# How many raw and split weights may be held: fixed numbers against the pages left free at each unit

## The chip, the cores and the metric

The kernel runs on one core of a Trainium2 chip. What counts is the device time of one execution in microseconds (us). Five engines matter: TensorE (PE) multiplies, VectorE (DVE) and ScalarE (ACT) prepare its operands and take its results, GpSimd (POOL) and SyncE (SP) issue transfers from memory (HBM) into the on-chip buffer. Each engine works through its own instructions in order and waits on semaphores for the others.

## The reference: what is computed

One layer of a streaming encoder over 256 tokens of width 2048, batch 1, all in float32:

```
x = LN(ALPHA * x + 0.5 * (silu(x @ w1) * (x @ w3)) @ w2)           first FFN, inner width 5632
proj = x @ w_in                                                   conv'd q, k; v; output gate; mLSTM gates;
                                                                  stick-breaking q, k, v; two branch gates ga, gb
y_m  = head_norm(mLSTM(q, k, v, gates)) * sigmoid(mo)             4 heads of 256
y_sb = stick_breaking(sq, sk, sv)                                 8 heads of 128
mix  = (sigmoid(ga) * (y_m @ w_up_m) + sigmoid(gb) * (y_sb @ w_up_sb)) @ w_out
x = LN(ALPHA * x + mix)
x = LN(ALPHA * x + 0.5 * second FFN)
x = x + sigmoid(x @ w_ple_gate) * (p @ w_ple_proj)
```

Nearly all of the arithmetic is products of the 256 rows of `x` with weight matrices. The weights are read from HBM once each, some 530 MB in all.

## The kernel before

**Weights and units.** A weight is a block of 256 rows by (mostly) 512 columns. It arrives as float32 in a *raw* page (512 KB, one load on SP's queue, L1251) and is split in two: ACT casts it to a rounded form, the high part (L1277), and DVE subtracts that from the raw values, which leaves the low part (L1281). The two parts are two *split* pages. A *unit* is the work of PE on one weight for 128 of the tokens: six matmuls of 128x128 by 512 columns, for each of the two row blocks high times high (L1333), high times low (L1334) and low times high (L1335). There are 1,528 units and 1,100 weights.

**Seven-product pairs.** Where two matrices with the same input are multiplied (w1 and w3; the two branch gates; halves of other parts of w_in), `seven` replaces eight block products by seven. Some of its weights are sums. A sum is made in place in a raw page, either by DVE (`plus`, L373) or by a transfer that POOL issues and that adds on landing (`plus_load`, L379); both are made from a raw page that an earlier weight of the pair has just been split from, so the addition cannot begin before that split. Each weight of such a pair has one unit; a plain weight (`group`) has two, one for each half of the tokens. The four pairs of the two branch gates are of this kind, like the nine pairs of each FFN.

**Pages.** All of this lives in one pool of 51 pages (`PAGES`): the residual (4 pages), the transposed activations in split form (`actT`, 2 token halves x 4 chunks = 8 pages for the plain form, 8 more for the sums that the seven products need), hidden chunks of the FFN (2 pages each), tiles of the mixer, the raws and the splits. A page that is given to a new tile cannot be written before the last reader of the old one is done; that wait sits on the engine or queue that writes first.

**Order.** The program is a list of units with plain functions between them. Main units (plain groups) and side units (seven-product pairs) are woven. The instruction streams are written in the order of this list: a clock of the builder, `sched.now`, goes forward by the units alone and sets when the smaller pieces of work (evacuations, transposes, attention steps) are written in between.

**How far ahead.** After each unit `splits_due` writes the splits of coming weights as long as fewer than a certain number are held; a split counts as held from the writing of its cast until its last unit. A weight that is needed and not yet split is split on the spot. Each `split_one` first writes the cast and the subtraction, then counts out the raw pages that this weight was the last to use, and then calls `loads`, which writes loads until a certain number of raws are held. The two numbers come from `HELD`, by the stretch of the program, and from `RAW_EDGE, SPLIT_EDGE` = 4, 11 near the two ends of an FFN and the mixer:

```
HELD = {"ffn": (11, 6), "mix": (6, 6), "woven": (9, 6), "wide": (11, 6), "late": (8, 5)}
while pos["load"] < most and pos["raw"] < (4 if pos["at"] < 6 else limits(pos["split"])[0]):     # loads
while pos["split"] < most and len(splits) < limits(pos["split"])[1]:                               # splits_due
```

"ffn" holds for both FFNs, "woven", "wide" and "late" for the three parts of the mixer's long middle, where the seven-product pairs of w_in run beside the rest, "mix" for what is left.

Of the kernel before, what the change touches and what calls it, by code (L numbers as in the profile page):

```python
# [24 lines left out]

PAGES = 51
TEMP_BUFS = 6


HELD = {"ffn": (11, 6), "mix": (6, 6), "woven": (9, 6), "wide": (11, 6), "late": (8, 5)}  # L30
RAW_EDGE, SPLIT_EDGE = 4, 11
EDGE = 6

# [1 line left out]
PSUM_BUFS = 8  # L35
# [151 lines left out]
    return [p[0] for p in pairs] + [p[1] for p in pairs]  # L187


@with_exitstack  # L190
def kernel(
    ctx: ExitStack,
    tc: tile.TileContext,
    x, p, ffn1_w1, ffn1_w3, ffn1_w2, ln1_g, ln1_b, w_in, b_gates_m, conv_m, norm_m,
    w_up_m, w_up_sb, w_out, ln2_g, ln2_b, ffn2_w1, ffn2_w3, ffn2_w2, ln3_g, ln3_b,
    w_ple_gate, w_ple_proj, out,
):
    nc = tc.nc
    x, out = x[0], out[0]
    p = p[0, 0]  # L200
    w_in, w_out, w_up_m, w_up_sb = w_in[0], w_out[0], w_up_m[0], w_up_sb[0]

    consts = ctx.enter_context(tc.tile_pool(name="consts", bufs=1))
    dram_pool = ctx.enter_context(tc.tile_pool(name="dram", bufs=1, space=bass.MemoryType.DRAM))
    page_pool = ctx.enter_context(tc.tile_pool(name="page", bufs=PAGES))
    temp_pool = ctx.enter_context(tc.tile_pool(name="temp", bufs=TEMP_BUFS))
    small = ctx.enter_context(tc.tile_pool(name="small", bufs=4))
    ps_pool = ctx.enter_context(tc.tile_pool(name="ps", bufs=PSUM_BUFS, space=bass.MemoryType.PSUM))
    ctx.enter_context(tc.manual_schedule())

    sched = Sched()
    temps = [0]
# [1 line left out]
    def temp():  # L214
        sched.until(lambda: temps[0] < TEMP_BUFS)
        temps[0] += 1
        return temp_pool.tile([P, COL], F32, name="temp", tag="temp")
# [44 lines left out]
    def load_x(c, t):  # L262
        nc.sync.dma_start(out=xres(t, c * COL), in_=x[t * P:(t + 1) * P, c * COL:(c + 1) * COL])
# [209 lines left out]
    class Norm:  # L473
        def __init__(self, g, b, act, scale, wait, away=None):
            self.g_in, self.b_in, self.act, self.scale, self.wait, self.away = g, b, act, scale, wait, away
            self.whole = set()
            self.stats, self.half = {}, {}
# [570 lines left out]
    def sb(*heads):  # L1048
        col0 = [(sq0 + h * DS, 2 * DS) for h in heads[::2]]
        return flat(group(w_in, range(0, D, 2 * P), col0, len(heads) * DS, x1T,  # L1050
                          lambda ps, t: sb_columns(ps, t, heads)))
# [33 lines left out]
    def half(g, h, last=False):  # L1085
        w, act = ((w_up_m, ymT), (w_up_sb, ysbT))[h]
        return flat(group(w, range(0, HM * DM, 2 * P), g * COL, COL, act, up_done(g, h, last)))

    def ups(g):
        return half(g, 0) + half(g, 1, True)  # L1090
# [17 lines left out]
    last = sb(14, 15)  # L1108
# [3 lines left out]
    late = [Mode("late")] + half(0, 1, True) + half(1, 1, True) + ups(2)  # L1112
# [114 lines left out]
    splits = {}  # L1227
    pos = {"load": 0, "split": 0, "at": 0, "raw": 0}

    def at_edge(j):  # L1230
        return any(-EDGE <= j - e < EDGE for e in edges)

    def limits(j):

        if at_edge(j):
            return RAW_EDGE, SPLIT_EDGE
        return HELD[[m for e, m in modes if e <= j][-1]]

    def pieces(j):
        return [slice(0, 1), slice(1, 2)] if j == 0 else [slice(0, 2)]  # L1240

    def loads(most=len(raws)):
        while pos["load"] < most and pos["raw"] < (4 if pos["at"] < 6 else limits(pos["split"])[0]):
            j = pos["load"]
            r = raws[j]
            r.tile = page_pool.tile([P, 2, COL], F32, name="raw", tag="page")
            for ks in pieces(j):
                at = 0
                for src in r.src:
                    n = src.shape[-1]  # L1250
                    nc.sync.dma_start(out=r.tile[:, ks, at:at + n], in_=src[:, ks])  # L1251
                    at += n
                if j == 0 and ks.start == 0:
                    load_x(0, 1)
            pos["load"] += 1
            pos["raw"] += 1
# [11 lines left out]
    def split_one():  # L1268
        j = pos["split"]
        w = weights[j]  # L1270
        make(j)
        assert w.made or not w.make
        r = w.raw.tile[:, :, :w.cols]
        splits[j] = [page_pool.tile([P, 2, COL], F32R, name="split", tag="page") for _ in range(2)]
        hi, lo = (h[:, :, :w.cols] for h in splits[j])
        for ks in pieces(j):
            nc.scalar.copy(hi[:, ks], r[:, ks])  # L1277
            make(j + 1)
            if weights[min(j + 1, len(weights) - 1)].made or not weights[min(j + 1, len(weights) - 1)].make:
                make(j + 2)  # L1280
            nc.vector.tensor_tensor(out=lo[:, ks], in0=r[:, ks], in1=hi[:, ks], op=ALU.subtract)  # L1281
        pos["split"] += 1
        for f in w.soon:
            assert f.raw.tile is not None
            f.make()
            f.made = True
        pos["raw"] -= len(w.frees)
        for r in w.frees:
            r.tile = None
        loads()  # L1290

    def splits_due():
        most = pos["at"] + 3 if pos["at"] < 8 else len(weights)
        while pos["split"] < most and len(splits) < limits(pos["split"])[1]:
            split_one()
            if at_edge(pos["split"]):
                break

    for c in range(4):
        if c == 0:  # L1300
            load_x(0, 0)
            loads(1)
        for t in range(TT):
            if c:
                load_x(c, t)
            sched.spawn(start(c, t), max(0.01 * t, 5.2 * c + 1.3 * t - 2.6))
        loads(2 * c + 2)
    sched.run()
    split_one()
    sched.now = 0.02  # L1310
    sched.run()
    splits_due()
    warm(WARM2)
    make_tri()
    for u in program:
        if isinstance(u, (Boundary, Mode)):
            continue
        if not isinstance(u, Unit):
            u()
            continue  # L1320
        sched.until(lambda: u.act.ready(u.chunk, u.tt))
        j = u.tile.index
        pos["at"] = max(pos["at"], j)
        while pos["split"] <= j:
            split_one()
        if u.start:
            u.acc["ps"] = ps_pool.tile([P, COL], F32, name="mm", tag="ps")
        ps = u.acc["ps"][:, :u.cols]
        a, w = u.act.tiles[u.chunk, u.tt], splits[j]
        for k in range(2):  # L1330
            hi, lo = a[:, 0, u.sub + k], a[:, 1, u.sub + k]
            first, last = u.start and k == 0, u.stop and k == 1
            nc.tensor.matmul(ps, hi, w[0][:, k, :u.cols], start=first, stop=False, skip_group_check=u.onto)  # L1333
            nc.tensor.matmul(ps, hi, w[1][:, k, :u.cols], start=False, stop=False, skip_group_check=u.onto)  # L1334
            nc.tensor.matmul(ps, lo, w[0][:, k, :u.cols], start=False, stop=last, skip_group_check=u.onto)  # L1335
        sched.now += 6 * 0.2161 * u.cols / COL
        u.tile.uses -= 1
        if u.tile.uses == 0:
            splits.pop(j)
        if u.stop:  # L1340
            u.done(ps, u.tt)
        sched.run()
        splits_due()
# [27 lines left out]
```

## Time and profile before

| | |
|---|---|
| three runs, median (lowest to highest) | 2167.77 us (2166.32 to 2170.53) |
| the profiled execution, its own time | 2172.74 us |
| its span on the core | 2171.1 us |
| PE busy in it | 2154.1 us (99%) |
| DVE, ACT, POOL busy | 1921.2 (88%), 1360.8 (63%), 227.8 us (10%) |
| granted clock of PE, mean | 0.999 |
| bytes moved | 540.16 MB, 249 GB/s over the span |

A busy share says how much of the span an engine had an instruction in work, not whether it was held up inside one; matmuls overlap, so that a busy PE is not yet a PE at its peak. A group of instructions is named by its line, engine and tiles; behind its count stand the busy time, the mean duration of one and the idle time of the engine just before them, with what ended most of that idle time. Two rows of L1333 belong to each unit, so the n-th pair of them dates the n-th unit.

### The profile page before, as it was taken

How to read it: one execution, taken by the hardware profiler on the slowest of the kernel's cores; microseconds unless marked ns; L12 is line 12 of the kernel's file. 1: busy time of each engine (PE TensorE's matmuls, PEld its weight loads, DVE VectorE, ACT ScalarE, POOL GpSimd, SP SyncE). 2: the span in 40 equal slices, each digit the busy share in tenths (PEclk: the TensorE clock that was granted, in tenths of full speed). 3: DMA queues.
4: the chain of work that ended last, by engine and by line, in shares of the span. 5: the costliest groups of instructions: out<-in, count | busy, mean ns of one | idle time of the engine just before them, and what ended most of it. 6: DMA issues, size and time to landing. Idle time of an engine off the chain costs nothing.

```text
span 2171.1 us, 27709 instructions
## 1 busy us (share of the span) xinstructions
PE 2154.1 (99%) x9774; PEld 1778.0 (82%) x9774; DVE 1921.2 (88%) x2122; ACT 1360.8 (63%) x1681; POOL 227.8 (10%) x194
## 2 busy tenths in 40 slices
PE   9999999999999999999999999999999999999999
PEld 7888888888888888888877888888888888887887
DVE  6899999999998898889889886799999999999974
ACT  7656666656665766678876563655656666556572
POOL 0111111111100000101110100011111111110000
PEclk9999999999999999999999999999999999999999
DMA  9899899999994667998988986679999999999642
GB/s 348 215 276 270 249 270 273 277 273 265 276 316 134 218 218 215 239 254 244 286 238 210 303 296 206 203 193 270 270 246 271 279 274 272 251 271 291 238 158 94
DMA packets 285355, 540.16 MB, mean 249 GB/s; under 512 B 17272, under 2 KB 34592, under 8 KB 285216
## 3 DMA queue, kind: packets, MB, share of 16 engines
q1 hardware_dynamic: 234624, 440.87, 59.8%
q0 software_dynamic: 50592, 97.53, 25.1%
q8 instruction: 76, 1.25, 0.2%
q14 instruction: 63, 0.52, 0.1%
HBM read 532.04 MB, written 6.29 MB: 248 GB/s over the span
## 4 chain that ended last, share of the span: by engine, by line
PE 87%; DVE 5%; DMA 3%; issue 3%; ACT 1%; POOL 0%; SPq 0%; DVEq 0%; POOLq 0%; ACTq 0%
PE mm L1334 28%; PE mm L1333 28%; PE mm L1335 28%; DMA raw<-in_ffn_w_dram 3%; DVE split L1281 3%; PE ms L300 1%; DVE raw L373 1%; ACT split L1277 1%; PE ms L526 0%; DVE temp L599 0%; POOL raw L379 0%; PE ms L913 0%; PE ms L928 0%; DVE big L651 0%; PE ms L991 0%
## 5 line engine op out<-in xcount | busy, mean ns | idle before, releaser
L1277 ACT CAST split<-raw 128x1024 fp32r<-128x1024 f32 (+1 forms) x1101 | 1099.4, 1043 | 538.4 <-DMA raw<-in_ffn_w_dram 194.2
L1281 DVE TENSOR_TENSOR split<-raw,split 128x1024 fp32r<-128x1024 f32 (+1 forms) x1101 | 1289.4, 1210 | 120.9 <-ACT split L1277 112.0
L1333 PE MATMUL mm<-split,actT 128*128 128x512 f32 (+1 forms) x3056 | 1199.2, 392 | 1.5 <-DVE big L427 1.4
L1334 PE MATMUL mm<-split,actT 128*128 128x512 f32 (+1 forms) x3056 | 1185.3, 388 | 4.2 <-DVE split L1281 4.2
L1335 PE MATMUL mm<-split,actT 128*128 128x512 f32 (+1 forms) x3056 | 1185.8, 388 | 0.6 <-DVE actT L307 0.6
L1334 PEld LDWEIGHTS mm<-split,actT 128*128 128x128 f32 x3056 | 574.9, 188 | 121.4 <-DVE split L1281 9.1
L1335 PEld LDWEIGHTS mm<-split,actT 128*128 128x128 f32 x3056 | 574.3, 188 | 120.8 <-DVE actT L307 1.4
L1333 PEld LDWEIGHTS mm<-split,actT 128*128 128x128 f32 x3056 | 574.8, 188 | 116.7 <-DVE big L427 1.6
L379 POOL DMA_DIRECT2D raw<-in_ffn_w_dram x140 | 169.8, 1439 | 1187.1 <-DVE split L1281 852.9
L373 DVE TENSOR_TENSOR raw<-raw 128x1024 f32<-128x1024 f32 x198 | 241.0, 1218 | 3.1 <-DMA raw<-in_w_in_dram 1.5
L379 POOL DMA_DIRECT2D raw<-in_w_in_dram x46 | 55.7, 1402 | 517.8 <-DVE split L1281 425.7
L651 DVE SCALAR_TENSOR_TENSOR big<-mm,big 128x512 f32<-128x512 f32 x112 | 76.2, 682 | 3.0 <-PE mm L1335 2.8
L302 ACT CAST actT<-ms 128x512 fp32r<-128x512 f32 x60 | 35.2, 587 | 66.8 <-PE ms L300 61.8
L599 DVE TENSOR_TENSOR temp<-mm,temp 128x512 f32<-128x512 f32 x108 | 73.0, 686 | 1.8 <-PE mm L1335 0.6
L307 DVE TENSOR_TENSOR actT<-ms,actT 128x512 fp32r<-128x512 f32 x60 | 41.0, 684 | 16.0 <-ACT big L306 11.6
L245 ACT ACTIVATE temp<-mm 128x512 f32<-128x512 f32 (+1 forms) x36 | 20.3, 570 | 48.2 <-PE mm L1335 48.2
L241 ACT ACT_TABLE_LOAD x34 | 43.6, 1283 | 0.6
L295 DVE TENSOR_TENSOR actT<-temp,actT 128x512 fp32r<-128x512 f32 x40 | 26.5, 687 | 17.4 <-ACT actT L294 17.3
L1193 DVE TENSOR_TENSOR temp<-temp,big 128x512 f32<-128x512 f32 (+1 forms) x10 | 5.8, 583 | 26.4 <-ACT temp L245 26.4
L294 ACT CAST actT<-temp 128x512 fp32r<-128x512 f32 x40 | 23.9, 620 | 8.0 <-DVE temp L318 7.4
L300 PEld LDWEIGHTS ms<-ident,temp 128*128 128x128 f32 x176 | 21.4, 140 | 8.0 <-DVE actT L307 2.9
L245 ACT ACTIVATE rstd<-mv,eps 128x1 f32<-128x1 f32 x6 | 1.8, 295 | 41.8 <-DVE mv L509 41.8
(137 smaller groups left out, 602.5 us busy)
## 6 DMA issues: line engine op xcount, KB each, us to landing
raw<-in_ffn_w_dram SPq DMA_DIRECT2D x527, 512.0 KB, 6.4
raw<-in_w_in_dram SPq DMA_DIRECT2D x144, 512.0 KB, 5.5
raw<-in_ffn_w_dram POOLq DMA_DIRECT2D x140, 512.0 KB, 10.1
raw<-in_w_in_dram POOLq DMA_DIRECT2D x46, 512.0 KB, 9.0
raw<-in_w_out_dram SPq DMA_DIRECT2D x32, 512.0 KB, 5.1
raw<-in_w_ple_gate_dram SPq DMA_DIRECT2D x32, 512.0 KB, 5.0
raw<-in_w_in_dram SPq DMA_DIRECT2D x56, 256.0 KB, 5.2
raw<-in_w_up_m_dram SPq DMA_DIRECT2D x16, 512.0 KB, 5.2
```

The source lines that it names most:

```text
L241: nc.scalar.preload_act_table_set(table[0])
L300: nc.tensor.transpose(ps[:, k], src[:, k * P:(k + 1) * P], ident[:])
L307: nc.vector.tensor_tensor(out=dst[:, 1], in0=ps[:], in1=dst[:, 0], op=ALU.subtract)
L373: nc.vector.tensor_tensor(out=out.tile[:, :, :cols], in0=a.tile[:, :, :cols], in1=b.tile[:, :, :cols], op=ALU.add)
L379: nc.gpsimd.dma_start(out=out.tile[:, :, :cols], in_=src, accum_op=ALU.add)
L599: nc.vector.tensor_tensor(out=out, in0=a, in1=b, op=op)
L651: nc.vector.scalar_tensor_tensor(out=xs, in0=ps, scalar=0.5, in1=xs, op0=ALU.mult, op1=ALU.add)
L1277: nc.scalar.copy(hi[:, ks], r[:, ks])
L1281: nc.vector.tensor_tensor(out=lo[:, ks], in0=r[:, ks], in1=hi[:, ks], op=ALU.subtract)
L1333: nc.tensor.matmul(ps, hi, w[0][:, k, :u.cols], start=first, stop=False, skip_group_check=u.onto)
L1334: nc.tensor.matmul(ps, hi, w[1][:, k, :u.cols], start=False, stop=False, skip_group_check=u.onto)
L1335: nc.tensor.matmul(ps, lo, w[0][:, k, :u.cols], start=False, stop=last, skip_group_check=u.onto)
```

## The change

The fixed numbers of `HELD` are raised for raws, to 16 in "ffn", "woven", "wide" and "late", and for splits in "late" from 5 to 6; "mix" and the edges stay. Beside them stands a new bound. The whole layer is first issued to a stand-in that computes nothing: `Dry` tiles, a `DryPool` for the other pools, and a `DryCore` whose every call only notes which pages it was given. From this `Pages` knows, for each page that is neither raw nor split, the first and the last unit in which it is touched. `settle` counts the pages in use at each unit and keeps as `room` what is left of the 51 at the fullest of five units, from the one before to three ahead. Then the layer is issued in earnest. Now `loads` stops, once five raws are held, when one more would make raws and split pages together exceed the room, and `splits_due` stops when two more split pages would. The splits that are needed on the spot are not bounded.

```diff
+AHEAD_UNITS = 4
-HELD = {"ffn": (11, 6), "mix": (6, 6), "woven": (9, 6), "wide": (11, 6), "late": (8, 5)}
+HELD = {"ffn": (16, 6), "mix": (6, 6), "woven": (16, 6), "wide": (16, 6), "late": (16, 6)}
...
+class DryCore:
+    def __getattr__(self, _):
+        return self
+    def __call__(self, *args, **named):
+        for a in (*args, *named.values()):
+            if isinstance(a, Dry) and a.page is not None:
+                self.pages.touch(a.page)
+
+class Pages:
+    def touch(self, n):
+        first, _ = self.spans[n] or (self.unit, None)
+        self.spans[n] = first, self.unit
+    def tile(self, shape, dtype, name, tag):
+        if self.pool:
+            return self.pool.tile(shape, dtype, name=name, tag=tag)
+        if name in ("raw", "split"):
+            return Dry()
+        self.spans.append(None)
+        return Dry(len(self.spans) - 1)
+    def settle(self, pool):
+        used = [0] * (self.unit + 4)
+        for first, last in self.spans:
+            for u in range(first, last + 1):
+                used[u] += 1
+        self.room = [PAGES - max(used[max(u - 1, 0):u + AHEAD_UNITS]) for u in range(self.unit + 1)]
+        self.pool, self.unit = pool, 0
+    def left(self):
+        return self.room[self.unit] if self.room else PAGES
...
+    pages = Pages()
+    layer(DryCore(pages), pages, *[DryPool() for _ in range(5)], *args)
...
+    pages.settle(pool)
+    layer(tc.nc, pages, consts, dram_pool, temp_pool, small, ps_pool, *args)
...
+    def full(more):
+        return pos["raw"] + 2 * len(splits) + more > page_pool.left()
+
     def loads(most=len(raws)):
         while pos["load"] < most and pos["raw"] < (4 if pos["at"] < 6 else limits(pos["split"])[0]):
+            if pos["raw"] >= 5 and full(1):
+                break
...
-        while pos["split"] < most and len(splits) < limits(pos["split"])[1]:
+        while pos["split"] < most and len(splits) < limits(pos["split"])[1] and not full(2):
             split_one()
...
         sched.now += 6 * 0.2161 * u.cols / COL
+        page_pool.unit += 1
```

No instruction of the computation is added or taken away; what changes is where in the streams the loads and the splits are written, and which pages they get.

More of the change, by code (lines that the diff above doesn't have):

```diff
@@ L187, in skewed, with __init__, __getitem__, _same @@
     return [p[0] for p in pairs] + [p[1] for p in pairs]
-@with_exitstack
-def kernel(
-    ctx: ExitStack,
-    tc: tile.TileContext,
+class Dry:
+    def __init__(self, page=None):
+        self.page = page
+    def __getitem__(self, _):
+        return self
+    def _same(self, *_, **__):
+        return self
+    rearrange = bitcast = broadcast_to = _same
+class DryPool:
+    def tile(self, *_, **__):
+        return Dry()
+class DryCore:
+    def __init__(self, pages):
+        self.pages = pages
+    def __getattr__(self, _):
+        return self
+    def __call__(self, *args, **named):
+        for a in (*args, *named.values()):
+            if isinstance(a, Dry) and a.page is not None:
+                self.pages.touch(a.page)
@@ new lines, with __init__ @@
+class Pages:
+    def __init__(self):
+        self.pool, self.unit, self.spans, self.room = None, 0, [], None
+    def touch(self, n):
[5 more added lines that the diff above has]
+        if name in ("raw", "split"):
+            return Dry()
+        self.spans.append(None)
[9 more added lines that the diff above has]
+        return self.room[self.unit] if self.room else PAGES
@@ new lines, with kernel @@
+@with_exitstack
+def kernel(ctx: ExitStack, tc: tile.TileContext, *args):
+    pages = Pages()
+    layer(DryCore(pages), pages, *[DryPool() for _ in range(5)], *args)
+    pool = ctx.enter_context(tc.tile_pool(name="page", bufs=PAGES))
+    consts = ctx.enter_context(tc.tile_pool(name="consts", bufs=1))
+    dram_pool = ctx.enter_context(tc.tile_pool(name="dram", bufs=1, space=bass.MemoryType.DRAM))
+    temp_pool = ctx.enter_context(tc.tile_pool(name="temp", bufs=TEMP_BUFS))
+    small = ctx.enter_context(tc.tile_pool(name="small", bufs=4))
+    ps_pool = ctx.enter_context(tc.tile_pool(name="ps", bufs=PSUM_BUFS, space=bass.MemoryType.PSUM))
+    ctx.enter_context(tc.manual_schedule())
+    pages.settle(pool)
+    layer(tc.nc, pages, consts, dram_pool, temp_pool, small, ps_pool, *args)
@@ L194, with layer @@
+def layer(
+    nc, page_pool, consts, dram_pool, temp_pool, small, ps_pool,
     x, p, ffn1_w1, ffn1_w3, ffn1_w2, ln1_g, ln1_b, w_in, b_gates_m, conv_m, norm_m,
@@ L197 @@
 ):
-    nc = tc.nc
     x, out = x[0], out[0]
@@ L201 @@
     w_in, w_out, w_up_m, w_up_sb = w_in[0], w_out[0], w_up_m[0], w_up_sb[0]
[L203 to L209, printed above, removed]
     sched = Sched()
```

## The prediction

> **What bounds the kernel now.** I read the page's busy shares first, then who PE waited for, then what the casts waited for, then the chain of waits, and last the windows of the stretches that the new bound touches.
>
> ```profile
> span 2171.1 us, 27709 instructions
> PE 2154.1 (99%) x9774; PEld 1778.0 (82%) x9774; DVE 1921.2 (88%) x2122; ACT 1360.8 (63%) x1681; POOL 227.8 (10%) x194
> L1281 DVE TENSOR_TENSOR split<-raw,split 128x1024 fp32r<-128x1024 f32 (+1 forms) x1101 | 1289.4, 1210 | 120.9 <-ACT split L1277 112.0
> L1334 PE MATMUL mm<-split,actT 128*128 128x512 f32 (+1 forms) x3056 | 1185.3, 388 | 4.2 <-DVE split L1281 4.2
> ```
>
> PE is idle for 2171.1 - 2154.1 = 17 us in all, and only 4.2 us of that is for a split. So whatever the change does to loads and splits, it can hardly gain more than 4 us; it can lose much more. Next, what the casts (L1277) waited for, and how long the two kinds of transfer take:
>
> ```profile
>   DMA raw<-in_ffn_w_dram: 194.2, 97
>   DVE raw L373: 185.7, 92
> ...
>   DMA raw<-in_w_in_dram: 12.1, 7
> ```
>
> ```profile
> raw<-in_ffn_w_dram SPq DMA_DIRECT2D x527, 512.0 KB, 6.4
> raw<-in_ffn_w_dram POOLq DMA_DIRECT2D x140, 512.0 KB, 10.1
> raw<-in_w_in_dram POOLq DMA_DIRECT2D x46, 512.0 KB, 9.0
> ```
>
> Only the FFN weights and w_in have pages that POOL adds to, and only they show up here with long waits; w_out, whose 32 weights are all plain, made no cast wait though only six raws were held there. I matched the n-th cast with the n-th weight: of the 104 waits in the two DMA rows all but three are for a page that POOL was still adding to; the row of L373 is DVE making its sums. A plain load is almost never late. More raws cure a wait that is not there: an addition cannot start before the weight ahead of it in the same page is split, however early its raw arrived.
>
> What covers those waits is the stock of splits. This is the chain of waits at one late addition:
>
> ```profile
> 1945.01 12.16 DMA raw<-in_ffn_w_dram
> ...
> 1957.27 1.06 ACT split L1277
> ...
> 1958.36 1.24 DVE split L1281
> 1959.59 0.04 issue
> 1959.64 0.50 PE mm L1334
> ```
>
> ```profile
> 1959.64 0.50 PE L1334 MATMUL mm<-split,actT 128*128 128x512 f32 x1 [0.42 <-DVE split L1281]
> ```
>
> From the start of the cast to the first product that needs the low part are 1959.64 - 1957.27 = 2.37 us with both engines free: the shortest lag there is. With six held, PE waited here for only 0.42 us after a transfer of 12.16 us. Matching the 1,101 rows of L1281 with the first L1334 of each weight, the low part is ready ahead of its use by a median of 4.2 us in 222:278, 4.5 in 278:305, 2.2 in 1839:1890, 6.5 in 836:932 and 3.0 in 1125:1204.
>
> **The change part by part.** *The stand-in* runs before the program is built and issues nothing. Zero.
>
> *Raws to 16, splits bounded by pages.* The new rule decides by who takes the last page. `loads` runs inside `split_one`, right after a raw is counted out, and refills until raws + 2 x splits equal the room; `splits_due` needs two free pages and comes after the next unit. So once 16 raws are there they stay: each raw used is replaced at once, and when the room falls it is the splits that shrink, to (room - 16) / 2 rounded down, at least one (the one split on the spot). Raws reach 16 early: in both FFNs and at the head of "woven" the room is 28 or more for long enough, and 16 + 2 x 6 = 28.
>
> The room, from the lifetimes in the issue order: in an FFN 4 residual pages, 16 of the input's two forms, 2 for each hidden chunk alive. With one to four chunks these are 22, 24, 26, 28 pages, the room is 29, 27, 25, 23, and the splits held are 6, 5, 4, 3. Before it was six throughout (11 + 12 = 23 pages). In the mixer the branch gates' tiles and the attention's outputs grow to 30 and 31 pages (units 791 to 842), 33 at the peak: room 20 to 21 and 18, splits 2 and 1. Dated by the pairs of L1333, these stretches hold so many casts (core 0: us, ACT busy (x), clock, DMA share, GB/s):
>
> ```profile
> 1093.00:1103.00 10.00, 4.11 (x4) 1.00 0.75 236
> 1113.00:1125.00 12.00, 7.01 (x7) 1.00 1.07 300
> 1017.00:1030.00 13.00, 4.86 (x5) 1.00 0.65 204
> 1087.00:1093.00 6.00, 3.63 (x4) 1.00 0.79 265
> 1103.00:1113.00 10.00, 3.13 (x3) 1.00 0.75 193
> 1125.00:1204.00 79.00, 42.43 (x42) 0.98 0.83 224
> 278.00:305.00 27.00, 16.09 (x17) 1.00 0.89 264
> 1644.00:1671.00 27.00, 15.78 (x16) 1.00 0.89 261
> 222.00:278.00 56.00, 32.13 (x32) 1.00 0.88 251
> 1839.00:1890.00 51.00, 25.58 (x26) 1.00 0.88 251
> 836.00:932.00 96.00, 48.98 (x49) 1.00 0.88 235
> 1240.00:1255.00 15.00, 8.08 (x8) 1.00 0.98 361
> ```
>
> One split held: rows 1 and 2, 11 weights. Two: rows 3 to 6, 54. Three in the FFNs: rows 7 and 8, 33; three in the mixer: 26 in four short stretches between 998 and 1213. Four in the FFNs: eight stretches of which 222:278 is the first and 1839:1890 the last, 229 in all; four in the mixer: six, 836:932 to 1240:1255, 91. Five: about 225. The rest keep six or are edges and "mix".
>
> *What one split fewer costs.* A weight takes 56 / 32 = 1.75 us of PE's time in the FFN and 79 / 42 = 1.88 in the mixer's tight stretch; each split fewer is written that much later against PE, with its cast, its subtraction and the additions that hang on it. The reserve shrinks by as much. What is then short is paid once per turn of the splits held, since a wait of PE gives all that are under way the same time.
>
> ```profile
> 222.00:278.00 56.00, 31.75 (x83) 15.40 (x82) 1.00 0.88 251
> 1125.00:1204.00 79.00, 41.41 (x104) 19.78 (x103) 0.98 0.83 224
> ```
>
> These are L1333 alone, two to a unit: 56 / 41.5 = 1.35 us a unit where PE runs undisturbed.
>
> - Four, FFN: 3.5 us off reserves of 4.2 at best and 2.2 at worst. Most weights still come in time, about a quarter are short by around 1 us. Between nothing (ACT and DVE catch up while PE waits) and 0.25 us a weight I take 0.10, nearer the median rows: 229 x 0.10 = 23.
> - Three, FFN: 5.25 off 4.5, short 0.75 to 1 in a turn of three, 0.3 each (0.1 to 1.0): 33 x 0.3 = 10.
> - Two, mixer: the next weight is written when one unit is left before it, 1.35 us, and its lag is at least 2.37: 1.0 us short for a weight of one unit. By the reserve: three or four fewer (five or six were held) at 1.88 are 5.6 off 3.0, short 2.6 per two, 1.3 each. Ends 0.5 (a two-unit weight in between covers it) and 1.8; I take 1.2: 54 x 1.2 = 65.
> - One: nothing runs meanwhile, so the whole lag, 2.37 (1.0 if pages happen to be free): 11 x 2.4 = 26.
> - Three and four, mixer: 26 x 0.2 = 5 and, off a reserve of 6.5, 91 x 0.02 = 2. Five: 225 x 0.01 = 2. Up to 1.0, 0.25 and 0.05 each.
>
> *Loads written earlier.* Up to five loads move ahead of small transfers on SP (norm vectors, pages put away and brought back). SP waits for pages anyway, and the one who frees them is PE:
>
> ```profile
> SPq L1251 <- PE mm L1335: 1078.0, 488, 11.2
> ```
>
> So the small transfers start when PE gets there, as before: zero, with a few microseconds if a norm vector came too late. POOL's additions keep their order and start later, with the split in front of them; that is in the reserve above. Evacuations on ACT and DVE now stand ahead of casts that used to precede them; free while the reserve lasts.
>
> *Sum.* 23 + 10 + 65 + 26 + 5 + 2 + 2 = 133 us, against the profiled execution's 2172.74: 2306. That execution is 5 us above the median of 2167.77, so 2301; I say **2300 us**. All low ends: 54 x 0.5 + 11 x 1.0 + 59 x 0.1 = 44, so 2212. All high ends: 54 x 1.8 + 11 x 2.4 + 59 x 1.0 + 320 x 0.25 + 225 x 0.05 = 274, so 2442.
>
> **The rivals.**
>
> *Only the mixer pays (2265).* With four or three splits ACT and DVE just run closer behind PE. For it: ACT is 63% busy and the reserve of four is on the median not used up. Against: DVE has little room, 1921.2 of 2171.1 overall. 65 + 26 + 5 + 2 = 98: 2172.7 + 98 - 5 = 2266.
>
> *PE's clock falls as well (2340).* The trace has one such case in the very stretch:
>
> ```profile
> 1152.91 0.89 PE L1021 MATMUL ms<-temp,big 128*128 128x256 f32 x4 [2.00 <-DVE temp L1012]
> ...
> 1154.00:1156.00 2.00, 2.00 (x7) 1.52 (x6) 1.24 (x3) 1.64 (x4) 0.00 (x0) 0.50 1.10 262
> 1156.00:1158.00 2.00, 2.00 (x8) 1.57 (x7) 1.08 (x2) 0.05 (x1) 0.00 (x0) 0.68 0.56 109
> ```
>
> A pause of 2.00 us was followed by half speed for some 3.4 us (the column behind POOL's is the granted clock: 0.50 for 2 us, then 0.68), 1.7 us of work lost. In the stretches of one and two splits, 130 us before and some 220 after, PE would be busy about 60% of the time, in pauses of 1 to 2.4 us. Those 220 us are 65 times 3.4 us; if two in five of these ran at half speed: 26 x 1.7 = 44, 2340. Against: there the lag sets the pace, and a slow PE waits less. [...]
>
> *The splits are not crowded out (2168).* Were the loads to stop short and leave six splits their pages, nothing would change: no wait for a plain load is there to remove. The arithmetic of room 25 and 16 raws speaks against it.
>
> *Faster (2163).* One mechanism: a raw that POOL adds to, or that it adds on, arrives earlier, so additions land earlier and PE's 4.2 us of waits for splits go. It decides only if the splits held stay at six where these waits are, at 600 to 640 and 1500 to 2010, mostly room 25 to 27. Above four splits' reserve no gain survives.
>
> **How the numbers follow.** 2300: 0.42. Only the mixer: 0.27. Clock: 0.20. Not crowded out: 0.05, of which 0.04 within the bound. Faster: 0.04. Left: 0.02, slower. A measurement of this kernel tells about 0.2%, some 4 us, from no change. The range 2205 to 2400 takes in the three slower cases but for their ends, and leaves out the two others and the all-high sum. Faster 0.04, same 0.04, slower 0.92.
>
> **What would show it.** Right: PE's wait for L1281 rises from 4.2 to over 100 us, most of it between 1000 and 1300 us; ACT's casts wait for PE's L1335 and no longer for DMA; the FFN windows with 25 and 23 pages of room hold fewer L1333 than 83 in 56 us, those with 29 as many as before; the clock column falls below 1.00 in the mixer. Wrong: if PE's idle time stays near 17 us, the splits were never short, and I misread who takes the last page; if the FFN loses more than the mixer, DVE has less to give than I took.

## The result, and the profile after

The changed kernel takes 2260.64 us (median; 2258.68 to 2264.72), the kernel before 2167.96 us in runs beside it: 1.0429 times as long, 95% interval 1.0410 to 1.0447. That is 93 us more. The forecast was 2300 us, in a range of 2205 to 2400.

The page of the changed kernel, its busy shares and its groups for the cast (now L1354) and the products (high by high L1410, high by low L1411):

```profile
span 2257.8 us, 27860 instructions
PE 2187.3 (97%) x9774; PEld 1776.7 (79%) x9774; DVE 1933.5 (86%) x2122; ACT 1383.8 (61%) x1681; POOL 228.0 (10%) x194
...
L1354 ACT CAST split<-raw 128x1024 fp32r<-128x1024 f32 (+1 forms) x1101 | 1118.5, 1044 | 551.4 <-PE mm L1411 176.7
...
L1411 PE MATMUL mm<-split,actT 128*128 128x512 f32 (+1 forms) x3056 | 1198.1, 392 | 53.4 <-DVE split L1358 52.4
L1410 PE MATMUL mm<-split,actT 128*128 128x512 f32 (+1 forms) x3056 | 1202.7, 394 | 9.6 <-ACT split L1354 9.4
```

The counts are those of before, the mean durations too, to about 1%. What changed is who waits. PE's waits (total, times, longest), the first row from the kernel before, where L1334 was the line of high times low:

```profile
PE mm L1334 <- DVE split L1281: 4.2, 7, 1.0
PE mm L1411 <- DVE split L1358: 52.4, 65, 2.8
PE mm L1410 <- ACT split L1354: 9.4, 10, 1.6
```

A wait for the subtraction that was 4.2 us in 7 pieces is 52.4 us in 65, and PE now even waits for the cast that comes before it. These waits are not the whole loss: PE's idle time grew from 17.0 to 70.5 us, by 53.5, while the span grew by 86.7. The other 33 us lie inside PE's busy time, which rose from 2154.1 to 2187.3 us for the same 9774 instructions. A part is the lower clock shown below (0.81 from 1118 to 1181 us). Another, by my estimate, is lost overlap: in a unit of 1.35 us a product starts every 1.35 / 6 = 0.23 us though each takes 0.39, so that a pause would also cost what the products around it overlap. From 1181 to 1279 us, at a clock of 1.00, PE was busy for 81.9 us with 328 instructions, where it had been busy for 76.1 with 331 in the same units before. How the 33 us divide was not measured.

The casts, in turn, wait much more for PE to give pages back and less for transfers (two rows of before, then four of the changed kernel):

```profile
ACT split L1277 <- PE mm L1334: 60.3, 47, 4.2
ACT split L1277 <- PE mm L1335: 44.1, 48, 3.4
ACT split L1354 <- PE mm L1411: 176.7, 173, 4.2
ACT split L1354 <- DMA raw<-in_ffn_w_dram: 107.4, 60, 3.9
ACT split L1354 <- DVE raw L445: 105.3, 61, 4.6
ACT split L1354 <- PE mm L1412: 91.6, 117, 3.5
```

Products with the low part of either factor (now L1411 and L1412) held up 95 casts for 104 us before; now it is 290 casts and 268 us. The pool is full, and the casts wait for its pages. That alone does not price the change: run e2_splits_first below has nearly as much of this wait and lost only some 9 us. What counts is whether PE waits in the end.

*Where the time went.* The pairs of L1410 date the units of the changed kernel as those of L1333 did before. Four stretches of the changed kernel follow: the first FFN with four splits held, then with three, then the mixer with one to two (units 772 to 791) and with two (791 to 842); the columns are the busy time of PE, PE's weight loads, DVE, ACT and POOL with their counts, the granted clock, the DMA share and GB/s:

```profile
221.30:279.80 58.50, 57.10 (x251) 46.07 (x250) 53.52 (x54) 34.70 (x36) 7.28 (x6) 1.00 0.85 246
279.80:308.00 28.20, 27.50 (x123) 21.84 (x121) 24.48 (x24) 17.05 (x18) 2.42 (x2) 1.00 0.86 241
1118.00:1181.00 63.00, 43.58 (x135) 30.17 (x136) 33.97 (x39) 26.88 (x37) 4.87 (x4) 0.81 0.40 111
1181.00:1279.00 98.00, 81.88 (x328) 58.61 (x328) 69.40 (x75) 50.54 (x58) 9.43 (x8) 1.00 0.72 197
```

The 251 products of the first row took 56 us before and 58.5 now. The units of the last two rows took 32 and 79 us before, 63 and 98 now; in the kernel before they are these windows:

```profile
1093.00:1125.00 32.00, 29.90 (x136) 24.23 (x135) 28.55 (x37) 22.61 (x31) 4.87 (x4) 1.00 0.87 246
1125.00:1204.00 79.00, 76.11 (x331) 61.90 (x331) 72.03 (x81) 54.09 (x67) 9.66 (x8) 0.98 0.83 224
```

In the third no engine is near its limit: PE busy 43.6 of 63, DVE 34, ACT 27, DMA at 0.40. What is missing is something to do while the next split is made. How one such wait comes about shows in the order of time:

```profile
1126.70 0.63 PE L1410 MATMUL mm<-split,actT 128*128 128x512 f32 x1
1126.94 0.51 ACT L1077 CAST actT<-temp 128x384 fp32r<-128x384 f32 x1 [3.80 <-PE mm L1412]
1126.94 1.29 DVE L499 TENSOR_TENSOR big<-mm,big 128x512 f32<-128x512 f32 x2 [2.60 <-PE mm L1412]
1128.26 0.69 DVE L505 SCALAR_TENSOR_TENSOR big<-big,mm 128x512 f32<-128x512 f32 x1
1128.87 1.22 DVE L1358 TENSOR_TENSOR split<-raw,split 128x1024 fp32r<-128x1024 f32 x1
1130.00 0.55 DVE L1078 TENSOR_TENSOR actT<-temp,actT 128x384 fp32r<-128x384 f32 x1
1130.12 1.06 ACT L1354 CAST split<-raw 128x1024 fp32r<-128x1024 f32 x1 [2.67 <-DVE split L1358]
1130.14 0.50 PE L1411 MATMUL mm<-split,actT 128*128 128x512 f32 x1 [2.81 <-DVE split L1358]
```

DVE waits 2.60 us for PE, then takes three results out (1.29 and 0.69 us), and only then comes the subtraction for the weight that PE already needs; PE waits 2.81 us. The results' instructions were written ahead of this subtraction; with more splits held the subtraction would have been written first (this is read from the order of the program, no trace shows it). A 128x512 product takes 0.63 us here (the row at 1126.70, where the granted clock is 0.50) and 0.39 on the mean of the span; of the clock more below.

Summed by stretch, by the dates of the units:

| units | splits held, changed kernel | lost against before, us |
|---|---|---|
| first FFN, 20 to 468 | 6, 5, 4, 3 | 11.8 |
| mixer, 597 to 772 | 2 to 6 | 13.6 |
| mixer, 772 to 791 | 1 and 2 | 31.1 |
| mixer, 791 to 842 | 2 (3 in seven units) | 19.9 |
| mixer, 842 to 886 | 3 to 6 | 4.3 |
| second FFN, 959 to 1528 | 6, 5, 4, 3 | 6.8 |

The profiled execution of before took 5 us more than the median, most of it in its second FFN. Against run e1_raws_back below, whose FFNs are issued with the same numbers held, the two FFNs lost 24 us and the mixer 72, together the 96 us between the two spans.

### The profile page after: what moved, and what is told of

The parts are those of the page before. It is cut to its first block, busy times and chain, and to the rows that moved or that the text cites. A ratio compares the mean times of both kernels' runs of the same rounds, so it can differ in the third digit from the quotient of the medians.

```text
span 2257.8 us, 27860 instructions
## 1 busy us (share of the span) xinstructions
PE 2187.3 (97%) x9774; PEld 1776.7 (79%) x9774; DVE 1933.5 (86%) x2122; ACT 1383.8 (61%) x1681; POOL 228.0 (10%) x194
## 5 line engine op out<-in xcount | busy, mean ns | idle before, releaser
L1354 ACT CAST split<-raw 128x1024 fp32r<-128x1024 f32 (+1 forms) x1101 | 1118.5, 1044 | 551.4 <-PE mm L1411 176.7
L1411 PE MATMUL mm<-split,actT 128*128 128x512 f32 (+1 forms) x3056 | 1198.1, 392 | 53.4 <-DVE split L1358 52.4
L1410 PE MATMUL mm<-split,actT 128*128 128x512 f32 (+1 forms) x3056 | 1202.7, 394 | 9.6 <-ACT split L1354 9.4
L1412 PE MATMUL mm<-split,actT 128*128 128x512 f32 (+1 forms) x3056 | 1188.4, 389 | 0.6 <-DVE actT L379 0.6
L1411 PEld LDWEIGHTS mm<-split,actT 128*128 128x128 f32 x3056 | 575.7, 188 | 205.1 <-DVE split L1358 94.6
L1410 PEld LDWEIGHTS mm<-split,actT 128*128 128x128 f32 x3056 | 576.0, 188 | 130.2 <-ACT split L1354 14.9
L1412 PEld LDWEIGHTS mm<-split,actT 128*128 128x128 f32 x3056 | 575.5, 188 | 117.1 <-DVE actT L379 1.4
L313 ACT ACT_TABLE_LOAD x34 | 43.6, 1283 | 0.6
L366 ACT CAST actT<-temp 128x512 fp32r<-128x512 f32 x40 | 23.9, 619 | 9.0 <-DVE temp L390 7.0
L499 DVE TENSOR_TENSOR big<-mm,big 128x512 f32<-128x512 f32 x30 | 20.5, 687 | 8.7 <-PE mm L1412 8.4
L317 ACT ACTIVATE temp<-ms,gbT 128x128 f32<-128x128 f32 x64 | 24.1, 460 | 5.5 <-PE ms L598 5.5
```

Source lines behind the costliest of these rows:

```text
L313: nc.scalar.preload_act_table_set(table[0])
L317: nc.scalar.activation(out, in_, func, **kw)
```

## The experiments

The theory on record is that the raws crowd the splits out, and that PE waits for what is then missing ("crowding"). Two rivals explain the same 93 us: that the bound by pages stops the splits too early whatever the raws do ("bound"), and that 16 raws cost time by themselves ("raws").

**The raws back to their old numbers, the bound kept** (e1_raws_back):

```diff
-HELD = {"ffn": (16, 6), "mix": (6, 6), "woven": (16, 6), "wide": (16, 6), "late": (16, 6)}
+HELD = {"ffn": (11, 6), "mix": (6, 6), "woven": (9, 6), "wide": (11, 6), "late": (8, 6)}
```

> The changed kernel with the raw limits of before (11, 9, 11, 8; splits in the late part 6), the page bound left in both places. Counted from the issue order, the FFNs then hold six splits throughout as before, and the tightest units (772 to 808) four instead of one or two. Theory 'crowding' (raws that take the pages of the splits cost the time): within 2163 to 2185, at most some 10 us lost around 1090 to 1150 us. Rival 'bound' (looking three units ahead stops splits too early, however many raws there are): stays above 2215, with a loss in the FFNs too. Rival 'raws' (16 raws themselves cost time, by more transfers at once): about 2168.

Measured: 2164.17 us, ratio to before 0.9988 (0.9979 to 0.9997). The loss is gone: with the old numbers of raws the bound costs nothing. "Raws" had forecast the same here; the next run separates it from "crowding". PE waited for the subtraction three times:

```profile
PE mm L1411 <- DVE split L1358: 1.7, 3, 1.1
```

**The raws at 16, the splits first** (e2_splits_first):

```diff
-        while pos["split"] < most and len(splits) < limits(pos["split"])[1] and not full(2):
+        while pos["split"] < most and len(splits) < limits(pos["split"])[1]:
```

> The changed kernel without the page bound on the splits; the raw limit of 16 and the page bound on the loads stay. By the issue order six splits are held everywhere, 11 to 16 raws in the FFNs and 6 to 16 in the mixer's long middle. Theory 'crowding': back to 2160 to 2172, all of the 93 us gone, PE's waits for the splits at 4 us or less. Rival 'raws': the 18 us lost in the two FFNs stay, since there are 12 to 14 raws where the changed kernel has 16: about 2185. If it is faster than before by over 4 us, more raws do help once the splits are left alone.

Measured: 2176.77 us, ratio 1.0045 (1.0030 to 1.0060). One condition takes back 84 of the 93 us, with the raw limit still at 16. That is mostly "crowding". But some 9 us are left over, outside what it expected though short of what "raws" did (2185), and they are not in the splits alone:

```profile
PE mm L1411 <- DVE split L1358: 5.4, 6, 1.4
PE ms L372 <- DVE actT L379: 2.0, 2, 1.1
PE ms L1093 <- DVE temp L1084: 1.9, 1, 1.9
```

The casts' waits for pages are nearly those of the changed kernel, 248 casts and 246 us. With six splits held PE hardly notices them:

```profile
ACT split L1354 <- PE mm L1411: 159.2, 142, 4.2
ACT split L1354 <- PE mm L1412: 87.2, 106, 3.4
```

**At least three splits** (e3_floor3):

```diff
-        while pos["split"] < most and len(splits) < limits(pos["split"])[1] and not full(2):
+        while pos["split"] < most and len(splits) < limits(pos["split"])[1] and not (len(splits) >= 3 and full(2)):
```

> The changed kernel, its page bound on the splits put aside while fewer than three are held. It touches only the mixer's units 715 to 848, where one or two were held; the FFNs are as in the changed kernel. 'Crowding': the 62 us lost in those units fall to the price of three, 0 to 0.3 us a weight over some 75 weights, so 2200 to 2225; PE's clock there is at 1.00 again. 'Raws': 12 to 16 raws are still held, so 2245 or more.

Measured: 2212.32 us, ratio 1.0211 (1.0195 to 1.0226). The third split, in place of some of the raws, is worth 48 us, nearly all in those units, and the granted clock stays at 1.00, as expected (1.000 on the mean of the profiled execution). Stretch by stretch the FFNs lost what they lost in the changed kernel, to about a microsecond; units 772 to 791 lost 5.5 us instead of 31.1, units 791 to 842 0.1 instead of 19.9.

**Four splits in the FFNs, 11 raws** (e4_ffn_four, from the kernel before):

```diff
-HELD = {"ffn": (11, 6), ...
+HELD = {"ffn": (11, 4), ...
```

> The kernel before with four splits instead of six in both FFNs and 11 raws as ever: the price of a split without any more raws. From the stretches of the changed kernel that hold four (some 15 us lost over about 260 weights, 0.06 each) the about 790 weights of the FFNs away from the edges should cost 25 to 55 us: 2193 to 2223. 'Raws': no loss, 2168. My prediction's 0.10 us a weight would give 2247.

Measured: 2205.22 us, ratio 1.0176 (1.0159 to 1.0193). No raw was added, and 39 us went: 39 / 790 = 0.05 us a weight. The wait is again that for the subtraction (as above, the listed waits are less than the loss):

```profile
PE mm L1334 <- DVE split L1281: 22.1, 27, 1.5
```

**Two splits in the late part of the mixer, 8 raws** (e5_late_two, from the kernel before):

```diff
-... "late": (8, 5)}
+... "late": (8, 2)}
```

> The kernel before with two splits instead of five in the late part of the mixer (58 weights in units 804 to 890), its 8 raws as ever and no page bound. The price of two splits apart from the many raws. 'Crowding': what the changed kernel lost with two held, 0.5 us a weight, so some 30 us: 2185 to 2205; with my prediction's 1.2 us it would be 2237. 'Raws' (the splits were short there because 16 raws held up transfers): 2166.

Measured: 2186.77 us, ratio 1.0094 (1.0080 to 1.0108). With 8 raws the loss is there too: 18.5 us by the dates of units 791 to 959, over 58 weights 0.32 us each.

**PE kept busy where one or two splits are held** (e8_kept_warm, from the changed kernel):

```diff
         page_pool.unit += 1
+        if 772 <= page_pool.unit < 800 and page_pool.pool:
+            warm(3)
```

> The changed kernel with three small products (128x128 of ones, results unused) on PE after each of the units 772 to 799, which changes no output. In the changed kernel that stretch ran with one or two splits held, lost 31 us by unit 791, and the granted clock was at half for 23.9 us in it. If the clock made a part of that loss: the clock stays at 1.00 and the time falls by 5 to 12 us, to about 2250. If the lag of the splits sets the pace whatever the clock: 2258 to 2275, the 84 small products costing up to 0.2 us each where PE was not waiting.

Measured: 2268.54 us, ratio to before 1.0467 (1.0451 to 1.0483), so 8 us slower than the changed kernel. The same stretch of time as in the third row of the changed kernel's windows:

```profile
1118.00:1181.00 63.00, 49.07 (x248) 39.73 (x248) 33.91 (x41) 24.78 (x34) 2.89 (x3) 0.95 0.41 111
```

The mean clock rose from 0.81 to 0.95, half-speed time fell from 0.19 x 63 / 0.5 = 23.9 us to 6 or 7, and units 772 to 791 lost 31.2 us (31.1 without the small products). The stretch gained nothing. That does not show that the half clock was free, because the small products cost time themselves: units 782 and 783, in which PE waits for nothing, took 2.06 us each with them and 1.36 without, and some 4 of the 8 us lie in units 791 to 800. From unit 773 to unit 778, where most of the half-speed time lay, the kernel did become quicker (first row the changed kernel, second this run):

```profile
1122.30:1145.10 22.80, 15.31 (x38) 10.73 (x38) 9.68 (x12) 5.30 (x8) 0.00 (x0) 0.63 0.26 85
1127.60:1147.80 20.20, 15.22 (x69) 12.49 (x69) 8.83 (x11) 5.34 (x8) 0.00 (x0) 0.83 0.28 83
```

Half speed lasted 0.37 x 22.8 / 0.5 = 17 us in the first row and 7 in the second. Ten microseconds less of it went with 2.6 us less time, so that the 23.9 us would have cost some 6 of the 93 (an estimate from these two rows; the small products may hide a little more). By this estimate PE mostly ran slowly through time in which it would have waited, but not for nothing: DVE waits for PE's products too, 2.60 us in the row at 1126.94. The clock did not reach 1.00 as expected.

**Seven splits and nine raws in the FFNs** (e6_ffn_9_7, from e1_raws_back):

```diff
-HELD = {"ffn": (11, 6), ...
+HELD = {"ffn": (9, 7), ...
```

> Run e1_raws_back (2164) with 9 raws and 7 splits in the FFNs instead of 11 and 6: the same 23 pages, two of them given to the splits. 'Crowding': PE's last waits for splits in the FFNs shrink, 2158 to 2164. If raws were of use: slower than 2166.

Measured: 2178.00 us, ratio 1.0049 (1.0037 to 1.0062). I had expected a small gain; the seventh split costs 14 us against e1_raws_back (the two raws fewer are no cause: the next run has fewer still and loses nothing). PE's waits point to the reason:

```profile
PE ms L372 <- DVE actT L379: 5.9, 6, 1.6
PE ms L372 <- DVE big L723: 4.4, 2, 2.7
PE mm L1411 <- DVE split L1358: 1.6, 3, 1.1
```

L372 is a transpose, in the FFNs mostly of hidden chunks. It waits for DVE to take results out, and not for a split. By the order of the program one more subtraction now stands ahead of those results; that this is the whole 14 us was not shown. The reserve is thus not to be made as large as possible: too small or too large, PE ended up waiting for DVE (22.1 us for the subtraction in e4_ffn_four, 5.9 and 4.4 for results here), which was busy for 88% of the span before.

**Eight raws everywhere** (e7_raws_eight, from e1_raws_back):

```diff
+HELD = {"ffn": (8, 6), "mix": (6, 6), "woven": (8, 6), "wide": (8, 6), "late": (8, 6)}
```

> Run e1_raws_back with 8 raws instead of 11 and 9 in the FFNs and the mixer, six splits everywhere. Run e2_splits_first held six splits with up to 16 raws and took 2177. If each raw beyond need costs something (its loads are in the way of others), 8 are faster than 11: 2156 to 2163. If the 12 us of e2_splits_first are a matter of filling the pool to the last page, 8 raws change nothing: 2162 to 2167. If raws arrive too late with 8: above 2168, with ACT's casts waiting for plain loads.

Measured: 2163.90 us, ratio 0.9981 (0.9973 to 0.9990). Eight raws do what eleven do. This is the best version found, together with e1_raws_back, from which it can't be told apart: 2 to 4 us below the kernel before.

**Thirteen raws, the splits first** (e9_first_thirteen, e2_splits_first with 13 for 16), and **eight raws in 48 pages** (e10_eight_tight, e7_raws_eight with `PAGES = 48`), to see what the 9 us of e2_splits_first are:

> Run e2_splits_first (six splits everywhere, loads bounded by the pages, 2177) with the raw limit at 13 instead of 16. It differs from that run only where there is room for more than 13 raws; in the tightest units of the mixer it is the same. If the 12 us that e2_splits_first lies above 8 or 11 raws come from raws beyond 13 (loads in flight in the way of POOL's additions): 2162 to 2168. If they come from refilling the pool to its last free page in the mixer, or from the raws falling to 6 there: 2172 to 2178.

> Run e7_raws_eight (8 raws, six splits, 2164) in a pool of 48 pages instead of 51: up to three pages fewer lie free in the FFNs while raws and splits stay the same; in units 715 to 842 of the mixer four or five splits are held instead of six. If free pages between the tiles matter: 2 to 6 us lost in each FFN, 2170 to 2178. If only the number of splits matters: the FFNs as in e7_raws_eight and at most 0.06 us a weight in the mixer, 2163 to 2168.

Measured: 2167.64 us, ratio 1.0000 (0.9991 to 1.0009), and 2172.95 us, ratio 1.0024 (1.0015 to 1.0033). Some 9 of the 13 us between e2_splits_first and e7_raws_eight go with the raws beyond 13, as the first part of the expectation had it. But three pages fewer cost 9 us too, at 8 raws and, in the FFNs, the same six splits; the two FFNs lost some 7 us of it (4 in units 98 to 468). So the pages that lie free matter by themselves. Whether raws beyond 13 cost anything else than free pages, the two runs don't say. This stays open. It concerns 0.4%.

## Why the prediction was right, and where its sizes were off

**The path.** The bound of what could be gained (PE's 4.2 us for splits) and the rule that lets the loads take the last page were right, and so were the numbers held in the FFNs: six, five, four and three are what the issue order of the changed kernel has. Runs e1_raws_back, e2_splits_first and e3_floor3 show the crowding from three sides; e4_ffn_four and e5_late_two show that the missing splits cost without any raw added. Most of the loss was forecast for the mixer, 98 of 133 us; it was 72 of 96. In the mixer's tightest units one step was wrong: by the issue order the raws do not stay at 16 there but fall to 14 in places, and five weights had one split held, not eleven. Of the signs, the FFN windows, the clock (0.81 from 1118 to 1181 us) and the time of the waits came as said (34.6 of the 52.4 us lie between 1000 and 1300). PE's wait did not reach 100 us, and casts still wait 107 us for the FFNs' transfers.

**The sum came out 40 us too high.** 133 us stood against 93. Term by term, by the prediction's own stretches, against the kernel before in the mixer and against e1_raws_back in the FFNs:

| term | forecast | measured |
|---|---|---|
| two held, mixer | 54 x 1.2 (0.5 to 1.8) = 65 us | 36 us: 19.9 over the 42 casts of 1125:1204, 0.5 each; 16.4 over the 12 others, 1.4 each; 0.32 each in e5_late_two |
| one held | 11 x 2.4 = 26 us | 23.5 us, 2.1 each |
| three held, FFN | 33 x 0.3 = 10 us | 1.2 us in each of two stretches of 16 weights: 0.08 each |
| four held, FFN | 229 x 0.10 = 23 us | 16 us over eight stretches: 0.07 each; 0.05 in e4_ffn_four |

The mis-sized term is "two, mixer": it is 29 of the 40 us, and all of that in one stretch, 1125:1204. For it I took 3.0 us of reserve, took 5.6 off it, and held the lag to be what it was while DVE was nearly full. It is not. In that stretch, 1181 to 1279 us in the changed kernel, DVE was busy for 69.4 of 98 us where it had been busy for 72.0 of 79, and from the start of a cast to the end of its subtraction (the n-th row of each matched) the median is 2.32 us, against 3.43 before. I read this as the queues of ACT and DVE running empty while PE waits, so that the next split is made in about the 1959.60 - 1957.27 = 2.33 us that cast and subtraction took with both engines free in the trace before. In the first FFN the same median fell from 3.34 to 2.91 us with four held and from 2.67 to 2.31 with three. This is not the whole account. In e4_ffn_four and e5_late_two, where no raw was added and a weight lost no more, that time did not shrink (3.48 us against 3.37 in units 98 to 468 with four held, 4.81 against 3.51 in units 804 to 886 with two); why so little was lost there stays open.

The agreement for "one held" is partly luck. Of the sixteen weights in units 772 to 791 five had one split held and eleven two, and both lost about 2 us each. With two held a weight thus cost 0.5 us in one place and 1.4 to 2 in another. The number held does not set the price alone; what else does was not separated.

**The rivals.** "Only the mixer pays" has the number (2265) and not the mechanism: the FFNs paid a quarter. "The clock falls as well": it fell, for 23.9 us, with no single pause longer than 2.81 us, as the row with 2.00 us in the trace before had suggested. Its price was some 6 us by the estimate above and not 44, mostly for the reason that the text gave against it, that a slow PE waits less. "Not crowded out" and "faster" were ruled out by the time itself and by PE's 52.4 us. That more plain loads held are of no use is borne out by e7_raws_eight: with 8 raws instead of 9 and 11 the time is the same.

**What I had not put down.** That more raws cost something even where the splits are left alone (9 us in e2_splits_first) stood in none of the cases; nor that a seventh split would be a loss.

## What to carry to other kernels

Where two stages of a pipeline share one pool, it matters less how much each may take than who is asked first: the stage that refills at once keeps the pages, and the one nearer to the busiest engine runs dry. Before a buffer is deepened, look in the list of waits for anything that waits for it; here plain loads made hardly anyone wait, and 8 held did as well as 11. Judge by the waits of the busiest engine: the casts waited for pages almost as long in a kernel that lost 9 us as in the one that lost 93. When you price a thinner reserve, do not simply carry over the lag measured at full load: here it went from 3.43 us, with DVE busy for 72.0 of 79 us, to 2.32, with 69.4 of 98. The cost of a missing split climbs steeply as fewer are held, and differs by place: 0.05 to 0.07 us a weight at four held, 0.3 to 2 at two.

## What was not expected of the hardware

In the changed kernel the granted clock fell to 0.50 four times between 1118 and 1181 us (at 1124.1, 1130.9, 1151.4 and 1171.9), with no wait of PE longer than 2.81 us. Windows of this kernel, each as long as the shortest stretch at half speed (3.4 us, 1124.1 to 1127.5) and in step with the changes of the clock (columns as above):

```profile
1117.30:1120.70 3.40, 2.21 (x9) 1.33 (x8) 1.49 (x3) 0.58 (x1) 0.00 (x0) 1.00 0.00 0
1120.70:1124.10 3.40, 0.64 (x3) 0.19 (x1) 3.37 (x4) 2.26 (x3) 0.00 (x0) 1.00 0.49 154
1124.10:1127.50 3.40, 2.93 (x6) 1.82 (x6) 0.81 (x2) 0.51 (x1) 0.00 (x0) 0.50 0.00 0
1127.50:1130.90 3.40, 0.76 (x3) 0.67 (x4) 3.02 (x5) 0.78 (x1) 0.00 (x0) 1.00 0.49 154
1130.90:1134.30 3.40, 2.59 (x8) 1.85 (x7) 1.20 (x2) 0.27 (x1) 0.00 (x0) 0.50 0.00 0
1134.30:1137.70 3.40, 1.72 (x4) 1.44 (x5) 1.62 (x2) 1.04 (x1) 0.00 (x0) 0.50 0.00 0
1137.70:1141.10 3.40, 2.87 (x7) 1.76 (x7) 1.23 (x1) 0.00 (x0) 0.00 (x0) 0.50 0.37 120
1141.10:1144.60 3.50, 3.50 (x10) 2.84 (x10) 0.00 (x0) 1.34 (x3) 0.00 (x0) 0.50 0.53 162
1144.60:1148.00 3.40, 2.46 (x9) 1.26 (x8) 1.23 (x1) 3.38 (x6) 0.00 (x0) 1.00 0.48 170
1148.00:1151.40 3.40, 1.72 (x6) 1.21 (x7) 2.36 (x2) 3.34 (x5) 0.00 (x0) 1.00 0.53 164
1151.40:1154.80 3.40, 3.00 (x9) 2.22 (x9) 1.69 (x2) 1.93 (x2) 0.00 (x0) 0.50 0.38 116
1236.70:1240.10 3.40, 1.67 (x6) 1.05 (x6) 3.37 (x5) 0.59 (x2) 0.00 (x0) 1.00 0.40 114
```

PE was busy for 2.21 of 3.4 us in the first row, and the next row is still at full speed; it was busy for 0.64 and 0.76 us in the second and fourth, and half speed follows each. It follows even the window of 1148.00, with 1.72 us of work, half of the window; after the one of 1236.70, with 1.67 us, full speed stayed (1.00 from 1240.10 to 1243.50). The window ahead of the fourth fall, from 1168.40, had 1.21 us. So half speed came here after windows of 3.4 us with 0.64 to 1.72 us of work in them, and the work in the window before does not settle it alone. What brings full speed back these rows don't settle (2.59 and 2.87 us of work at half speed did not, 2.93 did).
